# Prompt attention with negated scores, and with the two halves of its weights summed in one set of PSUM columns

## The chip, the cores and the metric

The kernel runs on one core of a Trainium2 chip. The time is the device time of one launch in microseconds (us), the median of several runs. The core's engines are named as the profile names them: PE (TensorE, matrix products), PEld (the loads of its stationary operand), DVE (VectorE), ACT (ScalarE), POOL (GpSimd) and SP (SyncE, which here issues nearly all transfers). Each engine works through its own queue in the order in which the program was written, and waits on semaphores for the others. PSUM is the memory into which PE writes its sums, in banks of 512 fp32 columns; SBUF is the memory that holds everything else.

## What is computed

One step of a two-layer decoder for a prompt of 1024 tokens and 8 sample tokens: attention in three dilated windows, a pooling mixer, and behind each of them a gated channel mixer. Only the attention of the prompt is touched by the change:

```python
s = jnp.einsum("nbqhd,nbkhd->nbhqk", qb, kb).astype(jnp.float32) * SCALE
s = s + bias[:, np.clip(rel, 0, SPAN)]
s = jnp.where(valid[None, :, None], s, NEG_INF)
m = jnp.max(s, axis=-1)
p = jnp.exp(s - m[..., None])
l = jnp.sum(p, axis=-1)
o = jnp.einsum("nbhqk,nbkhd->nbqhd", p.astype(v.dtype), vb).astype(jnp.float32)
...
w = l * jnp.exp(m - jnp.max(m, axis=0))
w = w / jnp.sum(w, axis=0)
return jnp.einsum("gbthd,gbth->bthd", o, w)
```

A query reads the 128 keys before it in its own residue stream and itself; the streams are cut into blocks of 128, so a block of queries sees its own block of keys and, where there is one, the block before.

## The kernel before

Tokens lie on the free axis in three chunks of 352, 336 and 344 columns. Every large product is taken in three passes: weights and inputs are each split into a rounded high part and its rest, both held as fp32r (`w_hi`, `w_lo`, `hh`, `hl`), and high by high, high by rest and rest by high are added in one PSUM bank (`accumulate`, line 116). The weight pieces stream in, ACT takes the high part (L95) and POOL the rest (L96).

The first stage, about 100 to 1345 us of the span, projects queries, keys and values for 24 units: 8 pairs of heads times three window groups g = 2, 1, 0 (`order`). While PE works on the 216 products of one unit, the attention of the unit before runs in small parts between them. The places are written out by hand in `attend`: for block i of a unit the scores stand at place 6i + 1 (`scores`), the transposed weights at 6i + 15 (`probs_t`), the product with the values at 6i + 24 (`pv`), and behind every second block its finishing at 6i + 26 (`finish_o`). A place is a group of three matmuls of the projection. `between` issues what is due; nothing moves at run time, so each engine's queue has a fixed order and whatever waits holds up all that stands behind it. Two more rows of tasks run at the same places: `extra` (the groups of a pair of heads are weighted and merged, `Merge`) and `behind` (the attention of the sample tokens, `Sample`).

The path of a block: PE makes the scores of both heads (tile `s`, one PSUM bank; L450 where the block sees one block of keys, L457 where it sees two). DVE adds the bias and takes the row maximum with one custom instruction per head and an instruction that reads its accumulator into the tile `st` (L459), then negates the two maxima into the tile `nm` (L461). ACT takes the exponential with `nm` as its bias (L463). PE transposes the weights (L471, L473) into the single-buffered PSUM tile `pt`; ACT takes their high part (L475) and DVE the rest (L476) into `phl`, which frees `pt`.

The product with the values (`pv_mm`, L483): the stationary operand holds the high part and the rest of the values of a head side by side, 64 columns each. The moving operand is the high part and the rest of the weights, one behind the other, so one matmul has 2 x 128 columns where a block gives to one block of queries ("narrow") and 2 x 256 where it gives to two ("wide"). The two parts land in columns of their own: the tile `o` of a head has 2 x 256 columns, a full PSUM bank, for two blocks of queries. The pool keeps 3 such banks, and a pair of blocks takes 2, one for each head. At the end of the pair ACT copies the half of the partitions that belongs to the values' other part (L501, 64 x 512 for each head) into `part`, DVE adds the two halves (L510, 64 x 512 for each head), and POOL adds the two sets of columns and puts them in token order into the row `og` of the unit (L518, 128 x 256).

The rest of the kernel, the output projection's second half, two channel mixers and the pooling mixer, is not touched.

Of the kernel before, what the change touches and what calls it, by code (L numbers as in the profile page):

```python
# [11 lines left out]
F32 = mybir.dt.float32  # L12
# [17 lines left out]
# how many cache tiles of the samples are under way  # L30
AHEAD = 2
LOADS = [.85, .85, .85]
# the order of the tiles of the output projection
OUT = [5, 6, 3, 2, 0, 1, 4, 7]
# the down-projections: their first tile, how many tiles they take, the weight pieces before them
# [3 lines left out]
def sub_blocks(w):  # L39
    """Equal parts of at most 128 columns."""  # L40
    n = next(n for n in (3, 4) if w % n == 0)
    return [(s, s + w // n) for s in range(0, w, w // n)]
# [3 lines left out]
def trunk(ctx: ExitStack, tc: tile.TileContext, a, out):  # L46
# [7 lines left out]
    pieces = [a["w_qkv"][i] for i in range(72)] + [a["w_o"][h, i] for h in range(2) for i in range(4)]  # L54

    # The channel mixers and the pooling mixer between them, in the order of the weight stream. Around the pooling mixer
    # the chunks of tokens run one behind the other, so that one is pooled beside the products of another.
# [9 lines left out]
    # From this piece on the parts of the output projection leave room for a third load.  # L67
# [61 lines left out]
    def out_terms(w, n, c, k0):  # L129
        """Half of the output projection: the pieces hold two tiles of four pairs of heads each."""  # L130
        c0, c1 = CHUNKS[c]
        at = [512 * (n % 2) + 128 * k for k in range(4)]
        return [(w[0][:, at[k]:at[k] + 128], w[1][:, at[k]:at[k] + 128], hh[:, k0 + k, c0:c1], hl[:, k0 + k, c0:c1])
                for k in range(4)]
# [40 lines left out]
    class Norm:  # L175
        def __init__(self, x, gain, c, place, engines):
            """x(k) is a tile of the residual; place(kind) gives room for a row of a chunk or its statistics; the
            squares add up on these engines in turn."""
# [8 lines left out]
        def square(self, k):  # L187
            """Squares a tile; the square before it is added, so that no engine waits for it."""
# [24 lines left out]
        def stats(self):  # L213
            """Reciprocal roots of the mean squares, tokens on partitions."""
            # The square root's table is loaded before it is needed.
# [10 lines left out]
            # a step of Newton's  # L226
# [26 lines left out]
        def steps(self, stages=None):  # L253
            """Everything behind the statistics; the stages of a tile one step apart."""
# [21 lines left out]
    # ================= projections and attention =================  # L276
    so = persist.tile([128, 8, NS], F32, name="so")
    with ExitStack() as ph:
# [8 lines left out]
        # Keys of a head twice, for the queries and their rests, next to their own rests over zeros.  # L287
# [36 lines left out]
        def tables():  # L324
            """Bias by distance: forwards for the prompt, with the mask around it, and backwards for the caches."""
            def step(g, tag, src):
# [3 lines left out]
                if src.start == 0:  # L330
                    nc.vector.tensor_add(masks[g], ps, masks[g])
# [13 lines left out]
        def stream(ap, g, t0, t1, reverse):  # L345
            """Columns of tokens t0..t1 where the residue streams lie one after another; keys run backwards."""
            d = DILS[g]
            v = ap.rearrange("p (r s) -> p s r", r=d)
            if reverse:
                v = v[:, ::-1, ::-1]  # L350
            return v[:, t0 // d:t1 // d, :]

        class Unit:
            """A pair of heads in a group."""

        def evacuate(u, which, ps, c):
# [4 lines left out]
            scale = 0.125 if which == 0 else 1.0  # L361
            nc.scalar.activation(stream(raw[:, :T], u.g, c0, t1, which > 0),  # L362
                                 ps[:, :w].rearrange("p (s r) -> p s r", r=DILS[u.g]), AF.Copy, scale=scale)
# [20 lines left out]
        def pack_q(u):  # L384
            """Queries of a head over their own rounding rests: 128 rows for one pass."""
# [12 lines left out]
        def pack_k(u):  # L398
# [8 lines left out]
            # The last keys come first, as the streams run backwards.  # L407
# [33 lines left out]
        def scores(u, i):  # L441
# [5 lines left out]
            nm = qp.tile([128, 2], F32, name="nm", tag="nm", bufs=2)  # L447
# [10 lines left out]
            for h in range(2):  # L458
                nc.vector.tensor_tensor_reduce(p[:, h, :w], s[:, h, :w], bias[:, h, :w], 1.0, -3e38,  # L459
                                               op0=ALU.add, op1=ALU.max, accum_out=u.st[:, i, h, 0:1])  # L460
            nc.vector.tensor_scalar(nm, u.st[:, i, :, 0], -1.0, None, op0=ALU.mult)  # L461
            for h in range(2):
                nc.scalar.activation(p[:, h, :w], p[:, h, :w], AF.Exp, bias=nm[:, h:h + 1],  # L463
# [15 lines left out]
        def pv_mm(u, j, b0, b1, first):  # L479
            """Adds keys of block j to queries of blocks j+b0 .. j+b1-1, apart for the two parts of their weights."""  # L480
            q = (j + b0) % 2
            for h in range(2):
                nc.tensor.matmul(u.o[h][:, :, 128 * q:128 * (q + b1 - b0)], u.v[j // 4][:, j % 4, h, :],  # L483
                                 u.pt[j][0][:, h, :, 128 * b0:128 * b1], start=first, stop=True, skip_group_check=True)

        def pv(u, j):
            first = j % 2 == 0
            if first:
                u.o = [app.tile([128, 2, 256], F32, name="o", tag="o", bufs=3) for h in range(2)]
# [4 lines left out]
            if j % 2:  # L494
                # The partial sums of the output projection take the room during the last attention.
                x = 512 * (j // 2 % 2)
                tmp = (part[:, 0, x:x + 512].rearrange("p (x q) -> p x q", x=2) if (u.hp, u.g) != order[23] else
                       qp.tile([128, 2, 256], F32, name="ot", tag="ot", bufs=1))
                u.tmp = tmp, u.o
                for h, (own, other) in enumerate(((A, B), (B, A))):  # L500
                    nc.scalar.activation(u.tmp[0][own], u.o[h][other], AF.Copy)  # L501

        def finish_o(u, i):
            """Adds the parts of weights and values of two blocks, in token order."""
# [3 lines left out]
            tmp, o = u.tmp  # L508
            for h, own in enumerate((A, B)):
                nc.vector.tensor_add(tmp[own], o[h][own], tmp[own])  # L510
            if u.g == 0:
                dst, split = u.og[:, 256 * i:256 * i + 256], "p q -> p q"
            elif u.g == 1:
                dst, split = u.og.rearrange("p (n q r) -> p r n q", n=2, r=4)[:, i], "p (n q) -> p n q"
            else:
                dst, split = u.og.rearrange("p (s r) -> p r s", r=16)[:, 4 * i:4 * i + 4], "p (n q) -> p n q"
            parts = [tmp[:, x] if u.g == 0 else tmp[:, x].rearrange(split, n=2 if u.g == 1 else 4) for x in range(2)]
            nc.gpsimd.tensor_add(dst, *parts)  # L518

# [17 lines left out]
        class Merge:  # L537
# [17 lines left out]
            def weights(self):  # L555
# [5 lines left out]
                nc.vector.tensor_max(mx, top[:, 0], top[:, 1])  # L561
                nc.vector.tensor_max(mx, mx, top[:, 2])
                nc.vector.tensor_sub(e, top, each(mx))
# [856 lines left out]
```

## Time and profile before

| | |
|---|---|
| median of 3 runs | 3011.26 us (3010.56 to 3012.93) |
| span of the profiled execution, first to last instruction | 3007.3 us |
| PE busy | 2796.5 us, 93% |
| DVE busy | 1649.7 us, 55% |
| ACT busy | 1273.2 us, 42% |
| POOL busy | 1241.8 us, 41% |
| mean granted clock of TensorE | 0.976 of full speed |

A profiled execution has no time of its own here besides its span; the 4.0 us between the span and the median lie around the first and the last instruction. The busy share is an average over stages that differ: the attention stage, the long stretches of the channel mixers, and the pooling mixer between them. Durations of matmuls in the trace include the way through the array, and successive ones overlap, so what a matmul costs is read from the distance between its start and the start of the next one.

### The profile page before, as it was taken

To read this page: it belongs to the slowest core of one execution; us is meant where nothing else is said; L and a number is where in the kernel's file an instruction comes from. 1 tells how busy PE (TensorE), PEld (TensorE's weight loads), DVE (VectorE), ACT (ScalarE), POOL (GpSimd) and SP (SyncE) were. 2 spreads that over 40 slices of the span, in tenths; PEclk is the share of its full clock that TensorE was granted. 3 is DMA by queue.
4 is the path that set the end of the run, shared out by engine and by line. 5 is a ranking of instruction groups with operands and counts; after the bars stand their busy time and mean duration, and the time that the engine had idled before them with its cause. 6 is when DMAs were issued, how large, how long until landed. Compare 5 with 4: busy or idle time off the path is not lost.

```text
span 3007.3 us, 45367 instructions
## 1 busy us (share of the span) xinstructions
PE 2796.5 (93%) x17677; PEld 2724.2 (91%) x17677; DVE 1649.7 (55%) x3338; ACT 1273.2 (42%) x2596; POOL 1241.8 (41%) x949
## 2 busy tenths in 40 slices
PE   7998999998989898899999999998797999999998
PEld 5988888888989798889999999998787999999998
DVE  6677767676777767766222222337977422223235
ACT  5565656565656555544312122224454221312222
POOL 4345554555354636444423232336543532323231
PEclk9999999999999999999999999999898999999999
DMA  3134332433232324356111111113225211111111
GB/s 114 54 86 115 82 85 78 109 100 89 70 111 82 103 54 127 130 146 54 63 44 50 44 48 50 47 66 110 88 88 60 90 50 43 50 50 43 50 43 60
DMA packets 190119, 227.38 MB, mean 76 GB/s; under 512 B 68736, under 2 KB 152560, under 8 KB 189904
## 3 DMA queue, kind: packets, MB, share of 16 engines
q1 hardware_dynamic: 189856, 224.47, 26.9%
q8 instruction: 139, 2.28, 0.3%
q14 instruction: 76, 0.62, 0.1%
q10 hardware_dynamic: 48, 0.02, 0.0%
HBM read 201.55 MB, written 23.34 MB: 75 GB/s over the span
## 4 chain that ended last, share of the span: by engine, by line
PE 50%; DVE 10%; ACT 2%; issue 2%; DMA 1%; POOL 1%; SPq 0%; DVEq 0%; ACTq 0%; POOLq 0%
PE mm L116 49%; DVE nm L461 1%; DVE conv L1108 1%; POOL w_lo L96 1%; DVE sums L1217 1%; DVE part L211 1%; DMA w_raw<-in_w_in 1%; DVE p L459 0%; DVE nrow L239 0%; ACT w_hi L95 0%; DVE hl L251 0%; DVE x L393 0%; ACT p L463 0%; DVE k L402 0%; DVE phl L476 0%
## 5 line engine op out<-in xcount | busy, mean ns | idle before, releaser
L116 PE MATMUL mm<-hh,w_hi 128*128 128x352 f32 (+2 forms) x4064 | 1347.5, 332 | 29.4 <-DVE conv L1099 9.7
L116 PE MATMUL mm<-hh,w_lo 128*128 128x352 f32 (+2 forms) x4064 | 1316.5, 324 | 5.7 <-POOL w_lo L96 5.5
L116 PE MATMUL mm<-hl,w_hi 128*128 128x352 f32 (+2 forms) x4064 | 1318.3, 324 | 3.4 <-DVE hl L251 3.2
L116 PEld LDWEIGHTS mm<-hh,w_hi 128*128 128x128 f32 x4064 | 780.6, 192 | 40.3 <-DVE conv L1099 10.2
L116 PEld LDWEIGHTS mm<-hl,w_hi 128*128 128x128 f32 x4064 | 780.6, 192 | 10.5 <-DVE hl L251 6.8
L116 PEld LDWEIGHTS mm<-hh,w_lo 128*128 128x128 f32 x4064 | 779.2, 192 | 7.2 <-POOL w_lo L96 7.2
L96 POOL TENSOR_TENSOR w_lo<-w_raw,w_hi 128x1024 fp32r<-128x1024 f32 x194 | 478.2, 2466 | 530.7 <-ACT w_hi L95 515.4
L1108 DVE SCALAR_TENSOR_TENSOR conv<-gate,convp,conv 128x1024 f32<-128x1024 f32 (+3 forms) x126 | 135.0, 1072 | 474.8 <-ACT conv L1106 463.2
L116 PE MATMUL mm<-gh,w_hi 128*128 128x352 f32 (+2 forms) x1056 | 338.8, 321 | 7.8 <-ACT gh L1100 7.6
L116 PE MATMUL mm<-gl,w_hi 128*128 128x352 f32 (+2 forms) x1056 | 339.0, 321 | 1.2 <-POOL gl L1101 1.2
L116 PE MATMUL mm<-gh,w_lo 128*128 128x352 f32 (+2 forms) x1056 | 338.5, 321 | 0.2 <-POOL w_lo L96 0.2
L1044 DVE TENSOR_TENSOR x<-x,mm 128x352 f32<-128x352 f32 (+2 forms) x312 | 159.0, 511 | 309.0 <-PE mm L116 308.8
L95 ACT ACTIVATE w_hi<-w_raw 128x1024 fp32r<-128x1024 f32 x196 | 205.5, 1051 | 242.4 <-PE mm L116 231.3
L463 ACT ACTIVATE p<-p,nm 128x128 f32<-128x128 f32 (+1 forms) x384 | 169.8, 443 | 296.3 <-DVE nm L461 286.1
L1101 POOL TENSOR_TENSOR gl<-conv,gh 128x352 fp32r<-128x352 f32 (+2 forms) x132 | 122.5, 939 | 269.4 <-ACT gh L1100 267.6
L116 PEld LDWEIGHTS mm<-gh,w_hi 128*128 128x128 f32 x1056 | 199.2, 189 | 8.6 <-ACT gh L1100 8.1
L96 POOL TENSOR_TENSOR w_lo<-part,w_hi 128x1024 fp32r<-128x1024 f32 x56 | 138.2, 2468 | 151.5 <-ACT w_hi L95 142.1
L116 PEld LDWEIGHTS mm<-gl,w_hi 128*128 128x128 f32 x1056 | 199.0, 188 | 1.8 <-POOL gl L1101 1.8
L476 DVE TENSOR_TENSOR phl<-pt,phl 128x512 fp32r<-128x512 f32 (+1 forms) x192 | 104.6, 545 | 173.8 <-ACT phl L475 172.5
L116 PEld LDWEIGHTS mm<-gh,w_lo 128*128 128x128 f32 x1056 | 199.2, 189 | 0.5 <-POOL w_lo L96 0.5
L362 ACT ACTIVATE raw<-mm 128x336 f32<-128x336 f32 (+1 forms) x216 | 144.2, 669 | 118.4 <-PE mm L116 115.8
L1090 ACT ACTIVATE gate<-mm 128x352 f32<-128x352 f32 (+2 forms) x132 | 60.0, 455 | 299.6 <-PE mm L116 299.6
(195 smaller groups left out, 3467.6 us busy)
## 6 DMA issues: line engine op xcount, KB each, us to landing
w_raw<-in_w_in SPq DMA_DIRECT2D x76, 512.0 KB
w_raw<-in_w_qkv SPq DMA_DIRECT2D x72, 512.0 KB
part<-in_w_in SPq DMA_DIRECT2D x38, 512.0 KB
w_raw<-in_w_out SPq DMA_DIRECT2D x36, 512.0 KB
x<-qd SPq DMA_DIRECT2D x48, 256.0 KB
kc<-in_cache_k SPq DMA_DIRECT2D x48, 256.0 KB
vc<-in_cache_v SPq DMA_DIRECT2D x48, 256.0 KB
x<-c_d SPq DMA_DIRECT2D x42, 256.0 KB
```

The source lines that it names most:

```text
L95: nc.scalar.activation(hi, raw, AF.Copy)
L96: (eng or nc.gpsimd).tensor_sub(lo, raw, hi.bitcast(F32))
L116: nc.tensor.matmul(ps, l, r, start=first and i == 0, stop=last and i == n - 1)
L211: self.engines[j].tensor_add(acc, acc, s[:, :self.w])
L362: nc.scalar.activation(stream(raw[:, :T], u.g, c0, t1, which > 0), ps[:, :w].rearrange("p (s r) -> p s r", r=DILS[u.g]), AF.Copy, scale=scale)
L461: nc.vector.tensor_scalar(nm, u.st[:, i, :, 0], -1.0, None, op0=ALU.mult)
L463: nc.scalar.activation(p[:, h, :w], p[:, h, :w], AF.Exp, bias=nm[:, h:h + 1], accum_out=u.st[:, i, h, 1:2])
L476: nc.vector.tensor_sub(phl[:, :, 1, :w], ps[:, :, :w], phl[:, :, 0, :w].bitcast(F32))
L1044: nc.vector.tensor_add(xT[ct][:, c0:c1], xT[ct][:, c0:c1], ps)
L1090: nc.scalar.activation(gate[:, 2 + s:2 + e], group(tiles8(w, c), c), AF.Copy)
L1101: nc.gpsimd.tensor_sub(self.gl[f][:, s:e], conv[:, s:e], self.gh[f][:, s:e].bitcast(F32))
L1108: nc.vector.scalar_tensor_tensor(conv[:, c0:t1], gate[:, j + c0:j + t1], cw[j], conv[:, c0:t1], op0=ALU.mult, op1=ALU.add)
```

## The change

It has two parts. First, the scores are kept with the opposite sign: the queries are scaled by -1/8 instead of 1/8 when they leave PSUM, the bias table is negated together with its mask, the running minimum takes the place of the maximum, and the exponential is taken with scale -1 and that minimum as its bias. The instruction that negated the maxima (L461) and its tile are gone. The merge of the groups takes minima and subtracts the other way round, with as many instructions as before.

Second, the high part and the rest of the weights are no longer moved in one matmul of 2 x 128 or 2 x 256 columns but in two of half the width, which add into the same columns. Both heads of a pair of blocks then fit into one bank. ACT copies 64 x 256 for each head, DVE adds 64 x 256 for each head and writes straight into `og` in token order, and POOL has nothing left to add there.

```diff
@@ evacuate
+            sign = -1.0 if which == 0 else 1.0
             nc.scalar.activation(stream(raw[:, :T], u.g, c0, t1, which > 0),
-                                 ps[:, :w].rearrange("p (s r) -> p s r", r=DILS[u.g]), AF.Copy, scale=scale)
+                                 ps[:, :w].rearrange("p (s r) -> p s r", r=DILS[u.g]), AF.Copy, scale=sign * scale)
@@ scores
-            nm = qp.tile([128, 2], F32, name="nm", tag="nm", bufs=2)
...
             for h in range(2):
-                nc.vector.tensor_tensor_reduce(p[:, h, :w], s[:, h, :w], bias[:, h, :w], 1.0, -3e38,
-                                               op0=ALU.add, op1=ALU.max, accum_out=u.st[:, i, h, 0:1])
-            nc.vector.tensor_scalar(nm, u.st[:, i, :, 0], -1.0, None, op0=ALU.mult)
+                nc.vector.tensor_tensor_reduce(p[:, h, :w], s[:, h, :w], bias[:, h, :w], 1.0, 3e38,
+                                               op0=ALU.add, op1=ALU.min, accum_out=u.st[:, i, h, 0:1])
             for h in range(2):
-                nc.scalar.activation(p[:, h, :w], p[:, h, :w], AF.Exp, bias=nm[:, h:h + 1],
+                nc.scalar.activation(p[:, h, :w], p[:, h, :w], AF.Exp, bias=u.st[:, i, h, 0:1], scale=-1.0,
                                      accum_out=u.st[:, i, h, 1:2])
@@ pv_mm
             q = (j + b0) % 2
             for h in range(2):
-                nc.tensor.matmul(u.o[h][:, :, 128 * q:128 * (q + b1 - b0)], u.v[j // 4][:, j % 4, h, :],
-                                 u.pt[j][0][:, h, :, 128 * b0:128 * b1], start=first, stop=True, skip_group_check=True)
+                for x in range(2):
+                    nc.tensor.matmul(u.o[:, h, 128 * q:128 * (q + b1 - b0)], u.v[j // 4][:, j % 4, h, :],
+                                     u.pt[j][0][:, h, x, 128 * b0:128 * b1], start=first and h + x == 0, stop=True,
+                                     skip_group_check=True)
@@ pv
-                u.o = [app.tile([128, 2, 256], F32, name="o", tag="o", bufs=3) for h in range(2)]
+                u.o = app.tile([128, 2, 256], F32, name="o", tag="o", bufs=3)
...
-                    nc.scalar.activation(u.tmp[0][own], u.o[h][other], AF.Copy)
+                    nc.scalar.activation(tmp[own], u.o[other, h], AF.Copy)
@@ finish_o
             for h, own in enumerate((A, B)):
-                nc.vector.tensor_add(tmp[own], o[h][own], tmp[own])
...
-            nc.gpsimd.tensor_add(dst, *parts)
+                nc.vector.tensor_add(dst[own], split(o[own, h]), split(tmp[own]))
```

The smaller edits that belong to the sign (the bias table, the memset of its unused half, the merge) are as the words above say, one instruction for one.

The queue of PE at a place in the middle of a unit of group 0, before, with `mm` the projection and `o` the product with the values:

```order
L116 MATMUL mm<-hh,w_lo 128x336
L483 MATMUL o<-phl,vhl 128x2x128 x2
L483 MATMUL o<-phl,vhl 128x512 x2
L116 MATMUL mm<-hh,w_hi 128x336
L116 MATMUL mm<-hl,w_hi 128x336
```

And with the change:

```order
L116 MATMUL mm<-hh,w_lo 128x336
L485 MATMUL o<-phl,vhl 128x128 x4
L485 MATMUL o<-phl,vhl 128x256 x4
L116 MATMUL mm<-hh,w_hi 128x336
L116 MATMUL mm<-hl,w_hi 128x336
```

The place is the same, the number of matmuls doubles, and each is half as wide; over the kernel 304 narrow ones become 608 of 128 columns, and 128 wide ones become 256 of 256 columns.

The queue of DVE in a unit of group 1, from the maxima of one block to the finishing of an earlier pair of blocks, before (`ISA` is the custom instruction of L459 or its accumulator read):

```order
L438 TENSOR_TENSOR vhl<-vt,vhl 128x8x64
L459 ISA p,st<-s,bias 128x256
L459 ISA st 128x1
L459 ISA p,st<-s,bias 128x256
L459 ISA st 128x1
L461 TENSOR_SCALAR nm<-st 128x2
L510 TENSOR_TENSOR part<-o,part 64x512 x2
L391 CAST x_594<-raw 64x512
L393 TENSOR_TENSOR x_594<-raw,x_594 64x512
L476 TENSOR_TENSOR phl<-pt,phl 128x2x128
```

And with the change (the names of two casts differ only by the shifted lines):

```order
L440 TENSOR_TENSOR vhl<-vt,vhl 128x8x64
L460 ISA p,st<-s,bias 128x256
L460 ISA st 128x1
L460 ISA p,st<-s,bias 128x256
L460 ISA st 128x1
L521 TENSOR_TENSOR x_2993<-o,part 64x256 x2
L393 CAST x_594<-raw 64x512
L395 TENSOR_TENSOR x_594<-raw,x_594 64x512
L476 TENSOR_TENSOR phl<-pt,phl 128x2x128
```

The negation is gone, the two adds are half as wide and write the unit's row; all else keeps its place.

## Rows read from the trace of the kernel before

**Rows 1.** Busy time of each engine, granted clock and transfers in three stretches: the attention stage and the two long stretches of the channel mixers. Columns as in the first line of the answer: us of the stretch, busy us and instructions of PE, PEld, DVE, ACT, POOL, then PE's clock, the DMA share and GB/s.

```profile
core 0: us, PE busy (x) PEld busy (x) DVE busy (x) ACT busy (x) POOL busy (x), PEclk, DMA share, GB/s
100.00:1345.00 1245.00, 1122.53 (x7221) 1069.14 (x7222) 890.30 (x2127) 717.63 (x1715) 605.77 (x413) 0.97 0.34 96
1413.00:2048.00 635.00, 635.00 (x4031) 635.00 (x4031) 188.53 (x286) 167.85 (x238) 218.62 (x192) 1.00 0.18 53
2320.00:2969.00 649.00, 648.34 (x4103) 648.10 (x4104) 203.87 (x287) 163.94 (x231) 213.36 (x184) 1.00 0.15 50
```

**Rows 2.** PE's groups by line and shape in the attention stage (100 to 1345 us): busy us, mean ns of one, then PE's idle time just before them and what ended it.

```profile
L471 PE MATMUL pt<-consts,p 128*128 128x128 f32 x376 | 84.4, 281 | 37.6 <-DVE phl L476 37.6
L483 PE MATMUL o<-phl,vhl 128*128 128x256 f32 x298 | 66.9, 293 | 30.7 <-DVE part L510 30.1
...
L483 PE MATMUL o<-phl,vhl 128*128 128x512 f32 x128 | 43.2, 409 | 6.8 <-DVE part L510 6.8
...
L434 PE MATMUL vt<-consts,raw 128*128 128x128 f32 x184 | 28.5, 277 | 14.3 <-DVE qr_sb L665 11.1 <-DVE spv_sb L765 2.9 <-DVE sacc L730 0.3
L760 PE MATMUL spv<-x,pst 128*16 128x256 f32 x144 | 25.5, 296 | 16.0 <-DVE so L787 13.9 <-DVE vhl L438 1.3 <-POOL x L778 0.5
```

**Rows 3.** Instructions in order of time around two waits of PE, 611.8 to 620.3 us, PE, DVE and POOL (start us, duration us, engine, line; in brackets the idle time before and what ended it).

```profile
611.81 2.88 DVE L393 TENSOR_TENSOR x<-raw,x 64x512 fp32r<-64x512 f32 x1
...
614.70 0.75 DVE L626 TENSOR_REDUCE sc<-kc 128x4 f32<-128x256 f32 x2
615.36 0.74 DVE L402 CAST k<-raw 64x512 fp32r<-64x512 f32 x1
616.02 0.68 DVE L476 TENSOR_TENSOR phl<-pt,phl 128x512 fp32r<-128x512 f32 x1
...
616.75 0.44 PE L471 MATMUL pt<-consts,p 128*128 128x128 f32 x2 [1.78 <-DVE phl L476]
...
618.41 0.40 PE L483 MATMUL o<-phl,vhl 128*128 128x512 f32 x1
...
619.13 1.40 DVE L510 TENSOR_TENSOR part<-o,part 64x512 f32<-64x512 f32 x2
...
619.86 0.51 PE L483 MATMUL o<-phl,vhl 128*128 128x512 f32 x1 [1.06 <-DVE part L510]
```

**Rows 4.** PE in order of time where nothing is waited for, 601.6 to 605.9 us, with the instruction that follows each: a wide product with the values, four transposes, a narrow product with the values.

```profile
601.66 0.62 PE L483 MATMUL o<-phl,vhl 128*128 128x512 f32 x2
602.12 0.31 PE L116 MATMUL mm<-hh,w_hi 128*128 128x336 f32 x1
...
603.74 0.27 PE L471 MATMUL pt<-consts,p 128*128 128x128 f32 x1
603.85 0.27 PE L473 MATMUL pt<-consts,p 128*128 128x128 f32 x1
603.96 0.27 PE L471 MATMUL pt<-consts,p 128*128 128x128 f32 x1
...
605.59 0.40 PE L483 MATMUL o<-phl,vhl 128*128 128x256 f32 x2
605.84 0.32 PE L116 MATMUL mm<-hh,w_hi 128*128 128x344 f32 x1
```

**Rows 5.** PE in order of time at two kinds of plain fp32 matmuls, with what follows: the bias table (384 and 136 columns, each matmul written as two records) and the sample tokens' own products (16 columns, 128 stationary columns; three matmuls, six records).

```profile
58.13 0.81 PE L329 MATMUL btp<-oh,rb 32*16 32x384 f32 x2
58.87 0.43 PE L116 MATMUL mm<-hh,w_hi 128*128 128x344 f32 x1
...
60.02 0.40 PE L329 MATMUL btp<-oh,rb 32*16 32x136 f32 x2
60.35 0.42 PE L116 MATMUL mm<-hh,w_hi 128*128 128x344 f32 x1
...
335.81 0.84 PE L728 MATMUL selfp<-selm,ss 32*128 32x16 f32 x6
```

**Rows 6.** DVE's groups by line and shape in the attention stage: busy us, mean ns, idle time before.

```profile
L510 DVE TENSOR_TENSOR part<-o,part 64x512 f32<-64x512 f32 x182 | 124.8, 686 | 7.1 <-ACT part L501 3.8
L461 DVE TENSOR_SCALAR nm<-st 128x2 f32<-128x2 f32 x186 | 104.4, 561 | 6.5
...
L476 DVE TENSOR_TENSOR phl<-pt,phl 128x256 fp32r<-128x256 f32 x101 | 42.8, 423 | 67.1 <-ACT phl L475 66.0
```

**Rows 7.** The negation's line and the adds' line by themselves: duration in ns, least, median and greatest.

```profile
L461 DVE TENSOR_SCALAR nm<-st x192: 169/170/2307, 79.9 to 1295.6; 128x2 f32<-128x2 f32 x192
...
L510 DVE TENSOR_TENSOR part<-o,part x184: 671/689/696, 97.0 to 1254.7; 64x512 f32<-64x512 f32 x184
```

**Rows 8.** Instructions in order of time at two long negations, all engines, 1012.8 to 1015.7 us and 1019.1 to 1022 us.

```profile
1012.86 2.35 POOL L594 TENSOR_TENSOR x<-x,x 128x1024 f32<-128x1024 f32 x1
...
1013.35 1.88 DVE L461 TENSOR_SCALAR nm<-st 128x2 f32<-128x2 f32 x1
1015.14 0.32 DVE L787 TENSOR_TENSOR so<-so,spt 64x4 f32<-64x4 f32 x2
...
1015.61 0.63 PE L760 MATMUL spv<-x,pst 128*16 128x256 f32 x4 [1.63 <-DVE so L787]
...
1019.17 2.37 POOL L96 TENSOR_TENSOR w_lo<-w_raw,w_hi 128x1024 fp32r<-128x1024 f32 x1 [0.95 <-ACT w_hi L95]
...
1019.88 1.70 DVE L461 TENSOR_SCALAR nm<-st 128x2 f32<-128x2 f32 x1
1021.49 0.40 DVE L765 TENSOR_TENSOR spv_sb<-spv_sb,spv 16x256 f32<-16x256 f32 x1
...
1021.94 0.33 PE L434 MATMUL vt<-consts,raw 128*128 128x128 f32 x1 [0.97 <-DVE spv_sb L765]
```

**Rows 9.** Groups by line and shape in the attention stage on ACT (the copy of a half, and a PSUM read of 256 columns) and on POOL (the adds that put `og` together).

```profile
L501 ACT ACTIVATE part<-o 64x512 f32<-64x512 f32 x182 | 107.9, 593 | 22.0 <-PE o L483 17.8
...
L475 ACT ACTIVATE phl<-pt 128x256 fp32r<-128x256 f32 x100 | 37.6, 376 | 31.8 <-PE o L483 24.8 <-PE pt L471 6.1
...
L518 POOL TENSOR_TENSOR x<-part 128x256 f32<-128x256 f32 x91 | 75.5, 829 | 169.2 <-DVE part L510 150.7 <-issue 12.4 <-PE s L450 5.4
```

More of the change, by code (lines that the diff above doesn't have):

```diff
@@ L330, in step @@
                 if src.start == 0:
-                    nc.vector.tensor_add(masks[g], ps, masks[g])
+                    nc.vector.scalar_tensor_tensor(masks[g], ps, -1.0, masks[g], op0=ALU.mult, op1=ALU.subtract)
                     nc.sync.dma_start(out=bias_tab[:, g], in_=masks[g])
@@ L353, in trunk @@
         class Unit:
+            pass
         def evacuate(u, which, ps, c):
@@ L494, in pv @@
             if j % 2:
-                x = 512 * (j // 2 % 2)
-                tmp = (part[:, 0, x:x + 512].rearrange("p (x q) -> p x q", x=2) if (u.hp, u.g) != order[23] else
-                       qp.tile([128, 2, 256], F32, name="ot", tag="ot", bufs=1))
+                x = 256 * (j // 2 % 2)
+                tmp = (part[:, 0, x:x + 256] if (u.hp, u.g) != order[23] else
+                       qp.tile([128, 256], F32, name="ot", tag="ot", bufs=1))
                 u.tmp = tmp, u.o
                 for h, (own, other) in enumerate(((A, B), (B, A))):
-                    nc.scalar.activation(u.tmp[0][own], u.o[h][other], AF.Copy)
+                    nc.scalar.activation(tmp[own], u.o[other, h], AF.Copy)
         def finish_o(u, i):
@@ L508, in finish_o @@
             tmp, o = u.tmp
-            for h, own in enumerate((A, B)):
-                nc.vector.tensor_add(tmp[own], o[h][own], tmp[own])
[L511 to L517, printed above, removed]
-            nc.gpsimd.tensor_add(dst, *parts)
+            if u.g == 0:
+                dst, split = u.og[:, 256 * i:256 * i + 256], lambda t: t
+            elif u.g == 1:
+                dst = u.og.rearrange("p (n q r) -> p r n q", n=2, r=4)[:, i]
+                split = lambda t: t.rearrange("p (n q) -> p n q", n=2)
+            else:
+                dst = u.og.rearrange("p (s r) -> p r s", r=16)[:, 4 * i:4 * i + 4]
+                split = lambda t: t.rearrange("p (n q) -> p n q", n=4)
+            for h, own in enumerate((A, B)):
+                nc.vector.tensor_add(dst[own], split(o[own, h]), split(tmp[own]))
         stat_d = {}
@@ L560, in weights @@
                 each = lambda t: t[:, None].to_broadcast([128, 3, 8, 2])
-                nc.vector.tensor_max(mx, top[:, 0], top[:, 1])
-                nc.vector.tensor_max(mx, mx, top[:, 2])
-                nc.vector.tensor_sub(e, top, each(mx))
+                nc.vector.tensor_tensor(mx, top[:, 0], top[:, 1], op=ALU.min)
+                nc.vector.tensor_tensor(mx, mx, top[:, 2], op=ALU.min)
+                nc.vector.tensor_sub(e, each(mx), top)
                 nc.scalar.activation(e, e, AF.Exp)
@@ L936, in trunk @@
                             b2 = qp.tile([128, 2, 128], F32, name=f"bias2_{x}")
-                            nc.gpsimd.memset(b2, NEG)
+                            nc.gpsimd.memset(b2, -NEG)
                             bias2.append(b2)
```

## Prediction

> **What bounds the kernel now.** I read the table of stretches first, since the 93% of PE's busy time is a mean over stages. In both long stretches of the channel mixers PE is busy without a gap and its clock is full [rows 1]; the change does not touch them, and nothing that it saves elsewhere can help there. The attention stage is different: of its 1245 us PE is busy for 1122.5, so it idles 122.5 us, and the granted clock is 0.97 of full speed [rows 1]. [...] DVE is busy for 890 us of the 1245 (72%), the other two for 58% and 49%: DVE is the engine whose backlog PE meets.
>
> The groups of PE by line say where the 122.5 us lie [rows 2]. Matmuls into `o` wait 37.5 us (30.7 + 6.8), nearly all until L510 on DVE has emptied a bank; transposes into `pt` wait 37.6 us until L476 on DVE has emptied that bank. The other 47.4 us are spread, most of it at the banks of the sample tokens and of the values' transposes, again ended by DVE. The order of time shows how such a wait comes about [rows 3]: DVE is behind after a long subtraction that ended at 614.69, does two reductions and a cast first, and empties `pt` from 616.02 on; PE starts 1.78 us late. Then the second head's product finds no free bank: L510 of the pair before starts only at 619.13, and PE waits 1.06 us.
>
> **The change part by part.** The base is the profiled execution: 3007.3 us of span, 4.0 us around it, 3011.3 together, which is the median.
>
> *PE gets more matmuls.* Where nothing waits, a narrow product with the values takes from 605.59 to 605.84, 0.25 us for two matmuls of 256 columns, and a wide one from 601.66 to 602.12, 0.46 us for two of 512 [rows 4]. The wide ones become four matmuls of 256 columns at 0.125: 0.50, so 64 x 0.04 = 2.6 us more. The narrow ones become four matmuls of 128 columns, and an fp32r matmul that narrow does not occur in the trace. Its price is bounded by three rows. Below: by columns alone, (0.230 - 0.125) / 256 = 0.41 ns a column, it would take 0.125 - 128 x 0.41 ns = 0.072 us. Between: four transposes of 128 columns start 0.11 us apart [rows 4], and the sample tokens' products, with 16 columns to move but 128 stationary columns to load, start (0.84 - 0.26) / 5 = 0.116 us apart, 0.26 being the mean of one [rows 5]; there the load of the stationary operand sets the pace, and the change loads as many columns. Above: plain fp32 costs (0.74 - 0.33) / (384 - 136) = 1.65 ns a column, 0.21 us for 128, and with what surrounds a lone one up to 0.31 [rows 5]. I take 0.115, because both rows with a full load and few columns stand there. A narrow product then takes 0.46 instead of 0.25: 152 x 0.21 = 32 us. With the wide ones PE has 34.5 us more to do, all on the path, since PE sets the end of this stage. The bounds: 152 x 0.04 = 6 us below, 152 x (4 x 0.31 - 0.25) = 150 us above.
>
> [...]
>
> *The banks of `o`.* A pair of blocks takes one of three banks instead of two. A bank then comes free a pair and more ahead of its next use, 28 places instead of 4 behind the finishing. The 37 us of waits there [rows 2] should go, all of them.
>
> *DVE does less.* The negation goes: 104.4 us in the stage, 561 ns each [rows 6]. Its median is only 170 ns [rows 7]; the mean is made by long ones, and these end with an instruction of POOL: 1013.35 + 1.88 and 1012.86 + 2.35 are both 1015.2, 1019.88 + 1.70 and 1019.17 + 2.37 both within 0.04 us of 1021.56 [rows 8]. What stands behind them is held up, and twice PE is idle at the end of that (1.63 and 0.97 us). The adds halve: 686 ns now, and a DVE instruction of 256 columns with PSUM among its inputs takes 423 [rows 6], so 192 x 0.26 = 50 us less. That a third of them write with a stride is not shown on DVE; between no cost and no saving I take no cost. So DVE has some 155 us less to do, 72% becomes about 60%. ACT's copies go from 593 ns to about 376 [rows 9], 42 us less, and POOL loses 96 adds of 829 ns, 80 us [rows 9]; neither engine bounds anything, but POOL blocks DVE less often. DVE now waits for what POOL waited for (that the row `og` is free), which was read out a whole unit earlier, so nothing new queues up behind it.
>
> *What that does to PE's other waits.* With DVE at 60% I let half of the waits at `pt` go: 20 of 37.6 us. They don't go entirely, because the transposes now also come without the pause that the wait at `o` gave DVE. Of the other 47.4 us a third goes, 16, since some of them end straight after a long negation. Bounds: nothing and 34, nothing and 35.
>
> [...]
>
> The sum: 34.5 - 37 - 20 - 16 - 17 = -55.5 us, so 3011.3 - 55.5 = 2956 us.
>
> **The rivals.**
>
> *A narrow matmul is dear.* If fp32r below 256 columns loses its single pass and costs what plain fp32 does, 0.21 us by the column plus some 0.015 of start, a narrow product takes 0.90 instead of 0.25: 152 x 0.65 + 2.6 = 101 us more PE work. More of the waits are covered then, so the gains are somewhat larger, 95 us: 3011 + 6 = 3017 us, slower. It decides from the point where the gains of 90 us are used up: (90 - 2.6) / 152 = 0.575 us more for a narrow product, that is (0.25 + 0.575) / 4 = 0.206 us for a matmul of 128 columns. For it: every fp32r matmul of the trace moves 256 columns or more, so the single pass is seen only there [rows 2, 4]. Against it: from 512 to 256 columns the price falls with the columns without a step [rows 4], and the transposes move 128 fp32 columns at 0.11 us. It gives 2980 to 3050 us, the upper end with 0.225 to 0.28 us for a matmul.
>
> *The lock moves on.* If the long negations are DVE waiting for POOL, the next instruction of DVE that needs the same access waits in their place; DVE then saves 192 x 0.17 = 33 us there, not 104, and its backlog stays. The waits at `o` go, but 10 us of them turn up at `pt`, and the clock gives 8 back: 34.5 - 37 + 10 - 8 = about 0, 3011 us. For it: the negations' ends fit POOL's. Against it: what follows the negation is mostly an instruction with PSUM among its inputs, as in both pieces [rows 8], and L510, which is such a one, keeps its duration from 671 to 696 ns [rows 7]. [...]
>
> *A narrow matmul is cheap.* At 0.072 us PE has 9 us more instead of 34.5: 2930 us.
>
> **How the numbers follow.** The forecast, 2956 us, has a chance of 0.46, and with its bounds 2925 to 2990. The dear matmul has 0.36, the lock that moves on 0.10 (2995 to 3025), the cheap one 0.08. About 0.2%, 6 us, is what a measurement of this kernel can tell from no change, so faster means below 3005. Faster: nearly all of the forecast (0.44), the cheap one (0.08), a third of the lock (0.04) and a quarter of the dear matmul (0.09): 0.65. Within 0.2%: 0.12, from the middle of the last two and the upper end of the forecast. Slower: 0.23, almost all the dear matmul. The range is 2925 to 3035: it leaves out the dear matmul's upper end and the tail below, about 0.15. The likeliest case's own range is 2925 to 2990.
>
> **What will show it.** The distance from the first of four narrow matmuls to what follows: 0.46 us by the forecast, 0.30 if cheap, 0.85 or more if dear. In PE's groups no idle time before the products with the values, about 17 us before the transposes. DVE's busy time in the attention stage near 740 us, its adds near 0.42 us. The stage itself ends some 55 us earlier while the long stretches of the channel mixers keep their length to a microsecond. The forecast is wrong if the narrow matmul's price is over 0.2 us, or if the waits at `pt` grow by what those at `o` lose.

## The result, and the profile after

The changed kernel takes 2930.32 us (median of 4 runs, 2928.91 to 2931.39) against 3010.91 us of the kernel before on the same chip: 80.6 us less, a ratio of 0.973 (95% interval 0.971 to 0.975). That is faster, inside the range, and 26 us below the forecast of 2956. Times here are medians of fast runs; of the four runs of the unread scalar instruction below, one of 5465 us was slow and is left out.

The table of stretches, with the attention stage now ending near 1265 us instead of 1345 (columns as in [rows 1]):

```profile
100.00:1265.00 1165.00, 1119.82 (x7660) 1091.55 (x7659) 754.51 (x1936) 684.20 (x1713) 531.60 (x318) 0.99 0.37 103
1335.00:1970.00 635.00, 635.00 (x4030) 635.00 (x4029) 189.31 (x285) 164.70 (x233) 219.88 (x189) 1.00 0.18 54
2240.00:2889.00 649.00, 649.00 (x4111) 648.76 (x4109) 202.34 (x285) 164.58 (x231) 212.61 (x183) 1.00 0.16 50
```

All of the gain lies in the attention stage; the two long stretches take 635 and 649 us as before [rows 1]. In the stage PE idles 1165 - 1119.8 = 45 us instead of 122.5, and the clock is 0.99 instead of 0.97. DVE is busy for 755 us instead of 890, POOL for 532 instead of 606.

PE's groups by line and shape in that stage (busy us, mean ns, idle time before, what ended it), the counterpart of [rows 2]:

```profile
L485 PE MATMUL o<-phl,vhl 128*128 128x128 f32 x596 | 85.1, 263 | 10.7 <-DVE phl L476 10.7
L471 PE MATMUL pt<-consts,p 128*128 128x128 f32 x374 | 82.0, 275 | 9.4 <-DVE phl L476 9.4
L485 PE MATMUL o<-phl,vhl 128*128 128x256 f32 x256 | 42.0, 286 | 0.0
L436 PE MATMUL vt<-consts,raw 128*128 128x128 f32 x184 | 27.5, 272 | 0.0
L764 PE MATMUL spv<-x,pst 128*16 128x256 f32 x144 | 23.3, 281 | 5.5 <-DVE so L791 5.5
```

The products with the values no longer wait for a bank at all: what is left there, 10.7 us, waits for the weights `phl` themselves. The transposes wait 9.4 us instead of 37.6, and the values' transposes nothing instead of 14.3.

PE in order of time at a narrow, a wide and again a narrow product where nothing waits, with what follows, the counterpart of [rows 4]:

```profile
584.01 0.56 PE L485 MATMUL o<-phl,vhl 128*128 128x128 f32 x4
584.40 0.38 PE L116 MATMUL mm<-hh,w_hi 128*128 128x352 f32 x1
...
587.47 0.64 PE L485 MATMUL o<-phl,vhl 128*128 128x256 f32 x4
587.95 0.32 PE L116 MATMUL mm<-hh,w_hi 128*128 128x336 f32 x1
...
590.77 0.65 PE L485 MATMUL o<-phl,vhl 128*128 128x128 f32 x4
591.25 0.37 PE L116 MATMUL mm<-hh,w_hi 128*128 128x344 f32 x1
```

The first narrow one takes 0.39 us, the wide one 0.48, the second narrow one 0.48 too. The first is the rule and the second an exception: of the 128 narrow products that stand alone between products of the projection, 116 take 0.39 or 0.40 us from the first matmul to what follows, four take 0.48, and eight hold a wait; the wide ones take 0.478 us in the median. Half the columns save less than a fifth of the time, and four matmuls of 128 columns take 0.16 us longer than two of 256 did before (median 0.237; the piece in [rows 4] shows 0.25). The price of 128 fp32r columns, which the trace of before did not hold, is 0.098 us here.

DVE's groups in the stage, the counterpart of [rows 6]:

```profile
L404 DVE CAST k<-raw 64x512 fp32r<-64x512 f32 x92 | 102.0, 1109 | 2.1
L521 DVE TENSOR_TENSOR x<-o,part 64x256 f32<-64x256 f32 x182 | 100.3, 551 | 6.9 <-ACT part L504 5.4
```

The adds take 551 ns, not the 423 that were reckoned, so they save 25 us and not 50.

### The profile page after: what moved, and what is told of

Read it like the earlier page. It is cut to its first block, busy times and chain, and to the rows that moved or that the text cites. A ratio compares the mean times of both kernels' runs of the same rounds, so it can differ in the third digit from the quotient of the medians.

```text
span 2927.1 us, 45930 instructions
## 1 busy us (share of the span) xinstructions
PE 2790.0 (95%) x18109; PEld 2742.4 (94%) x18109; DVE 1510.3 (52%) x3146; ACT 1240.5 (42%) x2596; POOL 1165.0 (40%) x853
## 4 chain that ended last, share of the span: by engine, by line
PE 78%; DVE 13%; ACT 3%; issue 3%; DMA 1%; POOL 1%; SPq 0%; DVEq 0%; ACTq 0%; POOLq 0%
PE mm L116 70%; PE o L485 2%; DVE k L404 2%; PE s L458 1%; PE pt L471 1%; DVE sums L1221 1%; DVE x L395 1%; DVE conv L1112 1%; PE s L451 1%; DVE nrow L239 1%; DVE sc L630 1%; DVE x L521 1%; DVE x L393 1%; PE spv L764 1%; PE vt L436 1%
## 5 line engine op out<-in xcount | busy, mean ns | idle before, releaser
L116 PEld LDWEIGHTS mm<-hh,w_hi 128*128 128x128 f32 x4064 | 773.5, 190 | 37.6 <-DVE conv L1103 10.2
L463 ACT ACTIVATE p<-p,st 128x128 f32<-128x128 f32 (+1 forms) x384 | 169.9, 443 | 204.2 <-DVE st L460 203.6
L1105 POOL TENSOR_TENSOR gl<-conv,gh 128x352 fp32r<-128x352 f32 (+2 forms) x132 | 122.5, 938 | 269.9 <-ACT gh L1104 269.9
```

What stands on the lines that cost most here:

```text
L116: nc.tensor.matmul(ps, l, r, start=first and i == 0, stop=last and i == n - 1)
L1105: nc.gpsimd.tensor_sub(self.gl[f][:, s:e], conv[:, s:e], self.gh[f][:, s:e].bitcast(F32))
```

## The experiments

All are compared with the kernel before on the same chip in the same job; its medians there were 3009.7 to 3012.9 us.

**The first part alone.** The kernel before with the negated scores; the product with the values is untouched.

```diff
-            nc.vector.tensor_scalar(nm, u.st[:, i, :, 0], -1.0, None, op0=ALU.mult)
...
-                nc.scalar.activation(p[:, h, :w], p[:, h, :w], AF.Exp, bias=nm[:, h:h + 1],
+                nc.scalar.activation(p[:, h, :w], p[:, h, :w], AF.Exp, bias=u.st[:, i, h, 0:1], scale=-1.0,
```

> The kernel before with the first part of the change alone: scores negated, no negation of the maxima; the product with the values as before. Theory (PE's waits end on DVE, and both DVE's load and the banks of o count): DVE's work falls by about 105 us, the waits at pt and the scattered ones shrink by about half, those at o by a third; 2975 us (2955 to 2990). Rival (only the banks count, DVE's load does not): 3011 us, within 8. Rival (the lock moves on): DVE saves 33 us only, 3000 us.

Measured: 2960.8 us, ratio 0.983 (0.982 to 0.985), 52 us less. PE's waits, longest first (us in total, times, longest):

```profile
PE o L482 <- DVE part L509: 40.5, 20, 4.4
PE pt L470 <- DVE phl L475: 20.5, 27, 1.6
PE spv L759 <- DVE so L786: 9.5, 7, 2.6
```

The time lies inside the theory's range. The waits at `pt` halve, but those for a bank of `o` stay at 40 us and do not fall by a third as expected. So a less loaded DVE does not cure them, and DVE's load matters nevertheless.

**The second part alone.** The changed kernel with the negation back in its place.

```diff
+            nc.vector.tensor_scalar(nm, u.st[:, i, :, 0], -1.0, None, op0=ALU.mult)
...
+                nc.scalar.activation(p[:, h, :w], p[:, h, :w], AF.Exp, bias=nm[:, h:h + 1],
```

> The second part alone: the two halves of the weights summed in the same columns, one bank for a pair of blocks; the negation of the maxima kept. Theory: PE has 35 us more to do, the waits at o go (37 us), DVE's adds halve, the waits at pt stay or shrink a little, clock gives some 10 back; 2985 us (2965 to 3005). Rival (only DVE's load counts): 3020 us, since 35 us of PE work stand against 25 us less of DVE's. Together with the first part alone: if the savings of the parts add up to less than 80 us, each makes room for the other's.

Measured: 2985.0 us, ratio 0.991 (0.989 to 0.993), 28 us less. 52 and 28 are 80, the whole of the change: in the time the parts neither need nor hinder each other. PE's waits:

```profile
PE pt L473 <- DVE phl L478: 20.2, 20, 2.6
PE spv L766 <- DVE so L793: 11.6, 11, 1.6
PE vt L436 <- DVE qr_sb L671: 10.8, 12, 1.4
PE o L487 <- DVE phl L478: 10.0, 10, 3.1
```

No wait for a bank of `o` is left, and some 25 us of PE's own work were bought with it.

**One bank, first try.** The changed kernel, three banks taken for a pair of blocks and the first of them used.

```diff
-                u.o = app.tile([128, 2, 256], F32, name="o", tag="o", bufs=3)
+                u.o = [app.tile([128, 2, 256], F32, name="o", tag="o", bufs=3) for _ in range(3)][0]
```

> The changed kernel with one bank for o instead of three (three are allocated for a pair of blocks and only the first is used), so that the next pair waits 4 places behind the finishing, as before the change; nothing else differs, DVE has the same work. Theory (the banks count): waits at o come back, 25 to 40 us with the clock, 2960 us (2945 to 2975). Rival (with DVE's load down the banks don't matter any more): 2930 us, within 6.

Measured: 2929.8 us, ratio 0.973. This looks like the rival, but it is void. In its order of time DVE is still emptying a pair's bank when PE begins the next pair:

```profile
156.14 1.23 DVE L521 TENSOR_TENSOR x<-o,part 64x256 f32<-64x256 f32 x2
...
156.44 0.64 PE L485 MATMUL o<-phl,vhl 128*128 128x256 f32 x4
```

Had the two been in one bank, PE would have waited, as it does in the next run. So the tiles that were never used evidently took no bank from the others.

**One bank in earnest**, by a bank of its own kind; the norms keep two of the others.

```diff
-                u.o = app.tile([128, 2, 256], F32, name="o", tag="o", bufs=3)
+                u.o = app.tile([128, 2, 256], F32, name="o", tag="o1")
...
-            return app.tile([128, 512], F32, name="nstat", tag=banks[0], bufs=3 if banks[0] == "o" else 1)
+            return app.tile([128, 512], F32, name="nstat", tag=banks[0], bufs=2 if banks[0] == "o" else 1)
```

> The changed kernel with one bank for o in earnest: a bank of its own kind, single, while the norms keep two of the three old ones. The first matmul of a pair of blocks now waits until DVE has finished the pair before, 4 places behind that finishing's place. Theory (banks count): waits at o come back, 20 to 35 us, 2955 us (2945 to 2970). Rival (with DVE's load down DVE is there in time): 2930 us, within 6.

Measured: 2974.9 us, ratio 0.987 (0.985 to 0.990), 45 us above the changed kernel. PE's waits:

```profile
PE o L485 <- DVE x L521: 49.3, 21, 5.0
PE pt L471 <- DVE phl L476: 9.4, 15, 1.0
```

The waits for the bank are back, more than expected, and those at `pt` are as in the changed kernel. With DVE at its lower load, three banks are still worth 45 us against one. One bank is harder than the layout before, where the first head's product found a bank free and only the second head's waited [rows 3].

**One bank and the negation**: the same edit on the second part alone.

> The second part of the change alone (the negation stays, DVE has some 110 us more to do than with both parts), with a single bank for o. Theory (a bank is only waited for as long as DVE is behind): the waits at o come back and more than in the run with both parts and one bank: 30 us above the 2985 us of the second part alone, 3015 us (3000 to 3030). Rival (the banks never mattered, only DVE's work): 2985 us, within 6.

Measured: 3038.0 us, ratio 1.009 (1.006 to 1.012): slower than before, and 53 us above the second part alone. The two further banks are worth 45 us with the lighter DVE and 53 with the heavier one; the runs of each kernel spread over some 15 us, so whether the two differ is not settled. With a single bank the second part loses 28 us.

**What POOL's adds were worth.** The changed kernel; DVE adds into the scratch row, contiguous, and POOL copies into token order.

```diff
-                nc.vector.tensor_add(dst[own], split(o[own, h]), split(tmp[own]))
+                nc.vector.tensor_add(tmp[own], o[own, h], tmp[own])
+            nc.gpsimd.tensor_copy(dst, split(tmp))
```

> The changed kernel, but DVE adds the halves side by side into the scratch row and POOL copies them into token order, as POOL wrote that order before the change. Theory (DVE's time and its blocking by POOL decide): POOL has some 96 x 0.8 = 75 us more and blocks DVE more often, DVE's adds fall from 0.55 to 0.42 us since they don't stride; the two nearly cancel, 2935 us (2925 to 2950). Rival (POOL's adds were a main part of what the change saved): 2955 us or more.

Measured: 2931.5 us, ratio 0.973: the same as the changed kernel. POOL was busy for 586 us of the stage instead of 532, and DVE for 744 instead of 755, so the two nearly cancel, as expected. To move this work from POOL to DVE was worth nothing on balance; what POOL's part costs by itself is not separated here. The adds themselves show why DVE's share was smaller than reckoned:

```profile
L521 DVE TENSOR_TENSOR part<-o,part 64x256 f32<-64x256 f32 x184 | 77.1, 419 | 7.1 <-ACT part L504 5.6
```

Contiguous they take 419 ns; into token order 551 in the mean.

**The price of a narrow matmul.** The changed kernel with the wide products cut into narrow ones, 64 times eight matmuls instead of four.

```diff
+                    for b in range(b0, b1):
+                        nc.tensor.matmul(u.o[:, h, 128 * (q + b - b0):128 * (q + b - b0 + 1)], u.v[j // 4][:, j % 4, h, :],
+                                         u.pt[j][0][:, h, x, 128 * b:128 * b + 128], start=first and h + x + b - b0 == 0, stop=True,
+                                         skip_group_check=True)
```

> The changed kernel with every wide product cut into narrow ones too: 64 products of four matmuls of 256 columns become eight of 128. Measures the price of a narrow matmul in the whole time. Theory (0.12 us each, paced by the load of the stationary operand, and paid in full because PE sets the end): 64 x (8 x 0.12 - 0.48) = 31 us more, 2961 us (2950 to 2968). Rival (narrow matmuls hide partly in waits that remain): under 10 us more. Rival (dear, 0.225 us): 84 us more.

Measured: 2952.0 us (2943 to 2956), ratio 0.979 (0.976 to 0.982), 22 us above the changed kernel. One of the eights, with what follows:

```profile
588.55 1.01 PE L486 MATMUL o<-phl,vhl 128*128 128x128 f32 x8
589.39 0.37 PE L116 MATMUL mm<-hh,w_hi 128*128 128x352 f32 x1
```

0.84 us for eight, 0.105 each; by the side of the 0.39 for four, each further one costs 0.113. 64 x (0.84 - 0.48) = 23 us, so within the spread of the runs the price is paid in full.

**An unread instruction where the negation stood.** The changed kernel with the negation's instruction, its result unused; and the same with a reduction of single values, again unused.

```diff
+            nc.vector.tensor_scalar(nm, u.st[:, i, :, 0], -1.0, None, op0=ALU.mult)
```

> The changed kernel with an instruction that nobody reads where the negation stood: DVE multiplies the two minima by -1 (128 x 2, SBUF to SBUF) into a tile that is not used. Theory (what the negation cost was DVE's time, most of it waiting for POOL): about 110 us of DVE time again, 560 ns each, and nearly all of the 50 us that the first part saved goes: 2970 us (2960 to 2985). Rival (the negation cost because the exponential waited for it, not by DVE's time): within 8 of 2930 us.

```diff
+            nc.vector.tensor_reduce(nm, u.st[:, i, :, 0:1], axis=mybir.AxisListType.X, op=ALU.add)
```

> The same place with an unread reduction of the same 128 x 2 values instead, a kind of instruction that by this theory does not wait for POOL: about 170 ns each, 33 us of DVE time, and a loss of 5 to 20 us: 2942 us (2935 to 2950). Rival (any DVE instruction there costs the same, since it waits for the accumulator): 560 ns each and 2970 us.

Measured: 2949.2 us with the scalar instruction (2944.0 to 2952.6, ratio 0.979, 0.977 to 0.981) and 2930.6 us with the reduction (0.973, 0.972 to 0.975). Duration of each by its line (least, median, greatest ns), the scalar one first:

```profile
L463 DVE TENSOR_SCALAR nm<-st x192: 168/170/2368, 79.8 to 1236.7; 128x2 f32<-128x2 f32 x192
```

```profile
L463 DVE TENSOR_REDUCE nm<-st x192: 154/155/157, 79.9 to 1214.5; 128x2 f32<-128x2 f32 x192
```

Same place, same data, same count: one is held up for as long as 2.4 us, the other never. Each of the 58 scalar ones that take over 0.4 us ends within 0.15 us of the end of an instruction of POOL, and so does each of the 57 such negations before the change. The reduction's 30 us of DVE time cost nothing, less than expected; the scalar one's 106 us, most of it standing still, cost 19, which is between the theory and the rival. It is not the 55 us between 2985 and 2930, so DVE's time is less than half of what the negation cost.

**The step itself.** The changed kernel, the reduction read by the exponential as its bias: a step more between minimum and exponential, but one that is not held up.

```diff
+            nc.vector.tensor_reduce(nm, u.st[:, i, :, 0:1], axis=mybir.AxisListType.X, op=ALU.add)
...
-                nc.scalar.activation(p[:, h, :w], p[:, h, :w], AF.Exp, bias=u.st[:, i, h, 0:1], scale=-1.0,
+                nc.scalar.activation(p[:, h, :w], p[:, h, :w], AF.Exp, bias=nm[:, h:h + 1], scale=-1.0,
```

> The changed kernel with the step between minimum and exponential put back, but by an instruction that does not wait for POOL: an unchanged copy of the two minima by a reduction of single values, read by the exponential as its bias. The unread scalar instruction cost 20 us, the unread reduction nothing, the negation itself 55 (2985 to 2930). Theory A (the missing 35 us are the exponential's wait for an instruction that is itself held up by POOL): with a step of 0.16 us that is not held up, 2934 us (2928 to 2940). Theory B (any step more between minimum and exponential costs, held up or not): 2950 to 2965 us.

Measured: 2939.9 us (2939.3 to 2940.8), ratio 0.976 (0.975 to 0.978), 10 us above the changed kernel, the upper end of theory A. The edit puts back more than a step: like the negation, the reduction stands behind the minima of both heads, while in the changed kernel the first head's exponential starts without the second head's minimum. The traces show the delay. From the read-out of the first head's maximum (or minimum) to the end of both exponentials a block took 1.81 us in the mean of 192 blocks before the change (at most 3.37), 0.94 with it (at most 1.19), and 1.39 in this run (at most 1.63). So about half of the 0.87 us between the first two comes back with a step that is never held up; the other half, 0.42 us, is there only where POOL holds the step up. In the time, 55 - 19 - 10 = 26 us are left for that half. This figure is a difference of three runs, good to some 5 us, and was not measured by itself.

**The free bank given to the transposed weights.** The changed kernel with two banks for `o` and two for `pt`.

```diff
-                u.o = app.tile([128, 2, 256], F32, name="o", tag="o", bufs=3)
+                u.o = app.tile([128, 2, 256], F32, name="o", tag="o", bufs=2)
...
-            ps = app.tile([128, 2, 256], F32, name="pt", tag="pt")
+            ps = app.tile([128, 2, 256], F32, name="pt", tag="pt", bufs=2)
```

> The changed kernel with the bank that the single banks of o leave free given to the transposed weights: two banks for o, two for pt. Theory: the 9 us of waits at pt for the bank go, those of the products with the values for phl itself stay; 2920 us (2912 to 2928). Rival (the waits at pt are DVE's backlog, and come back one instruction later at phl): 2930 us, within 5.

Measured: 2940.5 us, ratio 0.977 (0.975 to 0.978), 10 us above the changed kernel: neither theory. PE's longest waits:

```profile
PE o L485 <- DVE phl L476: 22.5, 10, 4.7
PE mt L578 <- DVE me L573: 8.8, 4, 2.2
```

The waits at `pt` are gone, and those for the weights at the next instruction have grown from 10.7 us to 22.5, in ten pieces of up to 4.7 us. The total of both hardly changes (20.1 and 22.5). The granted clock of the whole execution fell from 0.984 to 0.980, which is 0.004 x 2937 = 12 us and about the loss.

**A pause of the merge moved.**

```diff
-                    extra.extend([pause, pause, self.weights, self.rows])
+                    extra.extend([pause, self.weights, pause, self.rows])
```

> The changed kernel with one task of the merge moved: the weights of a pair of heads one slot (6 places) earlier, the pause that stood before them now between them and the transpose that needs them. PE waited 8.3 us four times for that step of DVE. Theory (PE is the end of the stage, so a wait of PE that goes is time that goes): 2922 us (2917 to 2926). Rival (the wait turns up at the next PSUM bank that DVE empties): 2930 us, within 4.

Measured: 2930.0 us, ratio 0.973 (0.971 to 0.974). The waits of 8.3 us before that transpose have shrunk to 1.1 us in the trace, but three of the four runs lie at 2929.6 to 2930.9 and one at 2924.5. As a gain over the changed kernel this is not settled. No version beat it clearly.

## Why the prediction held, and where its sizes were off

**PE's added work: the right order, over-sized by ten.** Reckoned 34.5 us at 0.115 us for a narrow matmul; the medians of the traces give 152 x (0.393 - 0.237) + 64 x (0.478 - 0.465) = 25 us, at 0.098 us. The row that was trusted, the pace of matmuls that load 128 stationary columns, 0.116 us [rows 5], holds inside a longer row of narrow matmuls, where each further one costs 0.113 us, but four by themselves cost less. The narrow product's 0.39 us lie between the 0.46 of the forecast and the 0.30 of the cheap rival, and far from the 0.85 of the dear one, which falls. That the cheap rival gave 2930 us, the time that was measured, is chance: its price was not reached, and the other gains were larger than it took them to be.

**The banks of `o`: right in mechanism.** Reckoned 37 us. With one part alone the waits stay (40 us) or go, as it should be, and one bank brings waits for a bank back, 49 us of them, and 45 us of time. They went as waits for a bank; 10.7 us of waits for the weights now show at the same instruction.

**DVE's load: the gain from the negation was under-sized, by a step that the prediction left out.** It took the negation as 104 us of DVE's time, 155 with the adds, and derived from that half of the waits at `pt` and a third of the others, 36 us. Those waits fell by 28 and by 22 us (47.4 to 25). The negation's time on DVE is worth only 19 of its 55 us. The rest goes to the path of a block: the exponentials stood behind a step that joined both heads (10 us) and that POOL held up (26 us, by difference). The prediction looked only at who waits on PE. ACT's exponentials over the whole execution, before and after (busy us, mean ns, idle time before and what ended it):

```profile
L463 ACT ACTIVATE p<-p,nm 128x128 f32<-128x128 f32 (+1 forms) x384 | 169.8, 443 | 296.3 <-DVE nm L461 286.1
```

```profile
L463 ACT ACTIVATE p<-p,st 128x128 f32<-128x128 f32 (+1 forms) x384 | 169.9, 443 | 204.2 <-DVE st L460 203.6
```

ACT's waits seemed to cost nothing since ACT is idle for two fifths of the stage, and most of them are still there; but what ACT makes there is what DVE and PE wait for later, and it now comes earlier.

**The adds: over-sized.** 25 us of DVE's time saved and not 50, as two thirds of them, and not a third, write with a stride. It can hardly have mattered: the 30 us of the unread reduction cost nothing. What ACT's shorter copies are worth was not tested by itself.

**The lock that moves on: fell, but for a small part.** The four groups of casts and subtractions that make the queries and keys took 260 us of DVE between 60 and 1340 us before and 247 after, though the casts of keys grew from 79 to 105 us. That comparison includes the adds that POOL lost. Where the negation alone goes, they grow: from 260 to 269 us with the first part alone, and from 241 to 247 from the second part alone to both. So of the negation's 107 to 113 us, 6 to 9 turn up there again. The pair of unread instructions shows that not every instruction of DVE is held up by POOL: at the same place and on the same values the scalar one took up to 2368 ns, the reduction 157 at the most. Why the one is held up and the other not, no run shows.

**The clock: under-sized by 8, and it did not follow PE's idle time.** No run shows the clock's terms as they stand in the sums, 17 us in the forecast and 8 us in the lock that moves on; they were estimates of the author. What the traces show in their place: the mean clock of the whole execution went from 0.976 to 0.984, by which some 3007.3 x 0.024 - 2927.1 x 0.016 = 25 us came back. A smaller idle time of PE did not by itself bring a higher clock: with the first part alone it fell from 122.5 to 80 us in the stage, and the clock was 0.973 to 0.975, no higher than the 0.975 to 0.978 of the kernel before beside it. What the clock follows here stays open.

**The sum.** PE's work +25, its idle time -77, the clock -25: -77 us of the 80. It is less exact than it looks. For the first part alone the same terms give -43 of idle time and +8 of the clock, -35 of the 48 us by which the span shortened, and the other 13 are not explained. PE's idle time counts only from the modelled end of a matmul, so the shortest waits are not in it. The forecast's -55.5 came from an added work that was 10 us too large and from gains at `pt`, at the other waits and by the clock that were 8, 6 and 8 us too small, partly balanced by the 11 us of new waits at the products with the values.

## What to carry to other kernels

A short instruction on the path between two engines can cost more than its work: look at its greatest duration (2307 ns for the negation), not its median (170 ns) [rows 7], at what its result releases two engines further, and at whether it makes one head wait for the other. Split accumulation so that a PSUM bank holds what comes free together, and price the narrower matmuls by rows that load as many stationary columns (0.116 us [rows 5]; 0.098 to 0.113 us measured here), not by the columns that they move (0.072 us as reckoned). Look at a single group of matmuls more than once before taking its price: one in thirty here took a fifth longer than the others. More buffers at one place are not a gain by themselves: if the producer is what is late, the wait moves one instruction on (with two banks for `pt` its 9.4 us went, and the waits at the products with the values grew from 10.7 to 22.5 us).

## What the runs showed of the hardware that was not expected

- A DVE add of 64 x 256 with one input in PSUM takes 419 ns into a contiguous row, and from 0.58 to 0.64 us where the writes step over 4 or 16 elements: the stride costs about 0.19 us.
- Four fp32r matmuls of 128 columns take 0.39 us and eight 0.84, four of 256 columns 0.48, each with 128 stationary columns: from four to eight, one of 128 columns costs 0.113 us, nearly as much as one of 256.
- Waits for DVE of nearly the same total went with different clocks: 20.1 us in pieces of up to 1.9 us with a mean clock of 0.984, 22.5 us in pieces of up to 4.7 us with 0.980. Whether the length of the pieces is the cause was not tested.
